# Second layer of a two-layer trunk: the order of the head pairs' rope transposes and of their attention, and TensorE's order by hand for all pairs

## The chip, the cores and the metric

The kernel runs on one core of a Trainium2 chip. The metric is the device time of one execution in microseconds (us). Three runs of the kernel before gave 768.90 to 769.38 us, median 769.24.

The engines have short names in the trace: PE is TensorE (matmuls and transposes), DVE is VectorE, ACT is ScalarE, POOL is GpSimd, SP issues DMAs.

## The reference

The program computes two layers of a sequence model on 512 tokens of width 1024. The first is a recurrent (mLSTM) layer with a memory cross-attention; the change does not touch it. The second is multi-head latent attention with 8 heads, again with a memory cross-attention. What matters here, of its core:

```python
kv = (rmsnorm(c_kv, kv_lat_norm) @ w_kv_b).reshape(bsz, s, B_HEADS, QK_NOPE + V_HEAD)   # 128 + 128
k = concat([k_nope, broadcast(k_pe)]); k = rmsnorm(k, k_gain)
k = concat([k[..., :QK_NOPE], rope(k[..., QK_NOPE:], positions)])
q = (rmsnorm(q_lat, q_lat_g) @ w_q_up).reshape(bsz, s, B_HEADS, QK_HEAD)                 # 128 + 64
q = rmsnorm(q, q_gain); q = concat([q[..., :QK_NOPE], rope(q[..., QK_NOPE:], positions)])
attn = chunk_causal_attention(q, k_sh, v_sh)       # blocks of 128 queries, chunk mask of 64
y_b = attn * silu(z)                               # z: a part of h @ w_in
x + concat([y_b, y_mem]) @ w_out
```

So each head's q and k has a part of 128 channels without position and a part of 64 channels that is rotated (rope).

## The kernel before

Products in float32 precision are made of three matmuls: an operand is split into a high part (ACT casts it, L130 or L133) and a low part (DVE subtracts, L131 or L134), and `prod` (L149 to L163) sums high x high, low x high (L157) and high x low (L162) in PSUM. Weights come by DMA into a buffer `wr` and are split into `wh` and `wl`, two buffers each. PSUM has four banks `acc` for products, two `att` for attention, two `tp` for transposes.

The second layer's heads are worked off in four pairs p = 0 to 3. `b_pair(p)` has three parts, and each yields between its steps. `b_kv(p)`: four products (one per 128 tokens, 6 matmuls of 512 columns) give k and v of two heads; DVE copies k (L928), ACT copies v and sums squares, and GpSimd makes the norm's factor and `krs`, the rotated part of k times that factor (L938). `b_q(p)`: four products of 9 matmuls of 384 columns; DVE copies the plain part (L978), ACT the part to be rotated into `qrs` (L979), and GpSimd rotates it in four operations on all tokens at once (L872 to L875) and makes `rqp`, the norm's factor as a power (L183). `b_z(p, c)` twice: the gate z, 24 matmuls of 512 columns in two halves of 12, then a silu. Between the steps of z six calls of `b_T` transpose on PE what attention needs: k and q of head 0 and 1 (L952) and the rope part of both heads (`h = 2`, L957). Each call takes one `tp` bank, which ACT and DVE read out; for the rope part each half takes one ACT operation (L960) and one or two of DVE (L962, L963).

`b_attn(p)` has nine steps: six of scores with softmax, for two heads and the query blocks (0, 1), (2) and (3); two steps after its scores a unit's probabilities are transposed (L1018); after the third unit of a head 20 value matmuls (L1031) and the gate. `weave(main, side, plan)` runs one step of main, then as many of side as the plan says.

The order on the engines comes from two sources. A scheduler sets it for all engines, except that inside `manual_schedule(engines={PE})` PE takes its instructions in the order in which the program writes them. Before, pairs 0 and 1 and the attention of pair 0 are outside of this block; pairs 2 and 3, the attention of pairs 1 to 3 and the out projection are inside. The four banks and the tile buffers are handed out by the scheduler as they come free.

Of the kernel before, what the change touches and what calls it, by code (L numbers as in the profile page):

```python
# [22 lines left out]
EPS = 1e-6  # L23
# [25 lines left out]
def chain(*gens):  # L49
    for g in gens:  # L50
        yield from g


def drain(g):
    for _ in g:
        pass
# [3 lines left out]
def trunk(ctx: ExitStack, tc: tile.TileContext, pv_d, pos_d, x_d, mem_d, memT_d, wmem_d, wg_d, wa_d, woa_d,  # L60
# [119 lines left out]
    def rpow(out, ss, mul, add, n):  # L180
        t = tiny([P, n])
        G.tensor_scalar(t, ss, mul, add, op0=ALU.mult, op1=ALU.add)  # L182
        G.tensor_tensor(out=out, in0=t, in1=mhalf[:, :n], op=ALU.pow)  # L183
# [721 lines left out]
    def b_z(p, c):  # L905
        d = pairs.setdefault(p, {})
        if c == 0:
            d["z"] = st([P, 2, S], ("z4", "mv")[p % 2])
        sz = d["z"]
        w = load(wb_d[8 + 2 * p + c], KT, P)  # L910
        ps = acc()
        yield from proj_T(w, hT, ps)
        silu2(sz[:, c], ps)
        yield

    def b_kv(p):
        d = pairs.setdefault(p, {})
        kns = st([P, NT, 256], "s4", 2)
        krs = s2([P, NT, P])
        d["v"] = vt = st([P, NT, 256], ("gt", "mkT")[p % 2])  # L920
        d["ks"] = kns, krs
        w = load(wkvb_d[p], 2, 512)
        ss = tiny([P, NT, 2])
        r2 = tiny([P, NT, 2])
        for t in range(NT):
            ps = acc()
            prod([(ps, lat(ckT, k, t), sub(w, slice(None), k), True) for k in range(2)], True, True)
            V.tensor_copy(kns[:, t], ps[:, 0:256])  # L928
            A.activation(vt[:, t], ps[:, 256:512], AF.Copy)
            for h in range(2):  # L930
                sqsum(kns[:, t, h * P:(h + 1) * P], ss[:, t, h:h + 1])
            if t < 3:
                yield
        V.tensor_tensor(out=ss, in0=ss, in1=sspe.unsqueeze(2).broadcast_to([P, NT, 2]), op=ALU.add)
        rpow(r2.rearrange("p a b -> p (a b)"), ss.rearrange("p a b -> p (a b)"), 1.0 / 192, EPS, 8)
        k4 = kns.rearrange("p t (h c) -> p t h c", h=2)
        V.tensor_tensor(out=k4, in0=k4, in1=r2.unsqueeze(3).broadcast_to([P, NT, 2, P]), op=ALU.mult)
        G.tensor_tensor(out=krs.rearrange("p t (h c) -> p t h c", h=2),  # L938
                        in0=kb.unsqueeze(2).broadcast_to([P, NT, 2, 64]),
                        in1=r2.unsqueeze(3).broadcast_to([P, NT, 2, 64]), op=ALU.mult)  # L940
        yield

    def b_T(p, name, h):

# [21 lines left out]
    def b_q(p):  # L966
# [6 lines left out]
        ssq = tiny([P, NT, 2])  # L973
        for t in range(NT):
# [7 lines left out]
            if t < 3:  # L982
                yield
        q4 = qrs.rearrange("p t (h c) -> p t h c", h=2)
        rope(q4, q4, 0, st([P, NT, 2, 64], "qt"),
             lambda i, a, b: tabs[:, i, :, a:b].unsqueeze(2).broadcast_to([P, NT, 2, b - a]))
        yield
        rpow(rqp.rearrange("p a b -> p (a b)"), ssq.rearrange("p a b -> p (a b)"), 1.0, 192 * EPS, 8)

    def b_attn(p):  # L990
        kn, qn, kh, qr, vt, sz, rqp = (pairs[p][n] for n in ("kn", "qn", "kr", "qr", "v", "z", "rq"))
# [53 lines left out]
            yield  # L1045

    def b_pair(p):
        yield from b_kv(p)
        yield from b_q(p)
        todo = [(n, h) for h in range(3) for n in "kq"]  # L1050
        for _ in chain(b_z(p, 0), b_z(p, 1)):
            yield
            b_T(p, *todo.pop(0))

    drain(b_pair(0))
    weave(b_pair(1), b_attn(0), (0,) * 5)
    x1b = []

    def residual():
# [6 lines left out]
        A.dma_start(out_d[t * P:(t + 1) * P, half * 512:(half + 1) * 512], o)  # L1066

    with tc.manual_schedule(engines={mybir.EngineType.PE}):
        weave(chain(*(b_pair(p) for p in range(2, 4)), residual(), out_proj(wob_d, yT, b_done)),
              chain(*(b_attn(p) for p in range(1, 4))), ((0,) * 5 + (1,) * 9) * 2)  # L1070


_OUTS = [((1, S, D), 'float32')]
# [101 lines left out]
```

## Time and profile before

| | |
|---|---|
| median of three runs | 769.24 us |
| the profiled execution | 769.35 us |
| its span, first to last instruction | 767.6 us |
| PE busy | 755.0 us, 98% |
| DVE, ACT, POOL busy | 63%, 53%, 14% |
| granted TensorE clock, mean | 1.0 |

The trace gives for every instruction its start and its duration. Matmuls overlap in the pipeline and their ends are modelled, so the time that one takes is read from start to start; a row of the timeline merges neighbours of one kind, with their count. An idle time in brackets is the time for which the engine stood before the row, and what released it.

The head pairs begin at about 538 us; the out projection begins at 685 us and ends the kernel.

### The profile page before, as it was taken

The numbers are of one execution on the slowest core, as the hardware profiler recorded it, in microseconds if no ns is written. First come the engines' busy times: TensorE is split into PE (matmuls) and PEld (weight loads), VectorE is DVE, ScalarE is ACT, GpSimd is POOL, SyncE is SP. The second block draws the span as 40 slices with busy tenths as digits, with TensorE's granted clock in tenths as the row PEclk, the third lists the DMA queues.
The fourth block names the chain that finished last, engine by engine and source line by source line (L and its number), as shares of the span: only waits on it lengthen the run. The fifth ranks groups of instructions, "written<-read, shape, count | busy, mean of one in ns | idle before, by whom it ended". The sixth has DMA issues, their size and how long they took to land.

```text
span 767.6 us, 10826 instructions
## 1 busy us (share of the span) xinstructions
PE 755.0 (98%) x3948; PEld 647.8 (84%) x3948; DVE 484.1 (63%) x945; ACT 409.4 (53%) x958; POOL 106.8 (14%) x159
## 2 busy tenths in 40 slices
PE   8999998999999999999999999999999999999998
PEld 6798887888888888888888887899888888888886
DVE  5743599547868836766434664566758697776422
ACT  6964557345446435536333658457856666644220
POOL 0131010010110101001001131020334230500000
PEclk9999999999999999999999999999999999999999
DMA  9523120322132222224443532121221111511241
GB/s 323 207 84 109 56 84 29 109 83 90 63 99 80 83 89 104 71 94 154 154 160 137 174 129 73 53 83 59 83 87 59 56 50 40 190 56 56 66 155 55
DMA packets 25909, 76.39 MB, mean 100 GB/s; under 512 B 3072, under 2 KB 3968, under 8 KB 25856
## 3 DMA queue, kind: packets, MB, share of 16 engines
q1 hardware_dynamic: 24144, 73.44, 28.4%
q10 hardware_dynamic: 1584, 2.25, 0.8%
q8 instruction: 31, 0.51, 0.3%
q14 instruction: 22, 0.18, 0.1%
q0 software_dynamic: 128, 0.01, 0.0%
HBM read 71.49 MB, written 4.19 MB: 99 GB/s over the span
## 4 chain that ended last, share of the span: by engine, by line
PE 85%; DVE 8%; ACT 3%; issue 1%; DMA 1%; POOL 0%; SPq 0%; ACTq 0%; DVEq 0%
PE acc L157 47%; PE acc L162 23%; PE att L157 3%; PE att L1031 2%; PE att L162 2%; DMA yTh<-in_wmem_dram 1%; DVE wl L131 1%; PE tp L1018 1%; DVE tiny L328 1%; ACT junk L187 1%; DVE kl L629 1%; ACT s L338 1%; PE tp L952 1%; PE att L715 1%; PE att L716 1%
## 5 line engine op out<-in xcount | busy, mean ns | idle before, releaser
L131 DVE TENSOR_TENSOR wl<-wr,wh 128x1024 fp32r<-128x1024 f32 (+5 forms) x117 | 136.2, 1165 | 152.9 <-ACT wh L130 126.7
L130 ACT ACTIVATE wh<-wr 128x1024 fp32r<-128x1024 f32 (+5 forms) x117 | 117.5, 1008 | 134.1 <-PE acc L157 123.8
L157 PE MATMUL acc<-wh,hTl 128*128 128x512 f32 (+3 forms) x320 | 113.3, 365 | 0.0
L157 PE MATMUL acc<-wh,hTh 128*128 128x512 f32 (+3 forms) x320 | 112.4, 367 | 0.3 <-ACT hTh L133 0.3
L157 PE MATMUL acc<-hTh,wh 128*128 128x512 f32 x256 | 101.8, 398 | 0.0
L157 PE MATMUL acc<-hTl,wh 128*128 128x512 f32 x256 | 100.3, 392 | 0.0
L157 PE MATMUL acc<-wh,yTh 128*128 128x512 f32 (+1 forms) x224 | 84.7, 382 | 0.0
L157 PE MATMUL acc<-wh,yTl 128*128 128x512 f32 (+1 forms) x224 | 84.5, 379 | 0.0
L162 PE MATMUL acc<-wl,hTh 128*128 128x512 f32 (+3 forms) x320 | 82.0, 364 | 0.0
L162 PE MATMUL acc<-hTh,wl 128*128 128x512 f32 x256 | 69.8, 392 | 0.0
L157 PEld LDWEIGHTS acc<-wh,hTh 128*128 128x128 f32 x320 | 59.1, 188 | 9.4 <-ACT hTh L133 0.6
L157 PEld LDWEIGHTS acc<-wh,hTl 128*128 128x128 f32 x320 | 59.6, 188 | 8.7 <-DVE hTl L134 0.2
L162 PEld LDWEIGHTS acc<-wl,hTh 128*128 128x128 f32 x320 | 56.5, 188 | 8.6
L162 PE MATMUL acc<-wl,yTh 128*128 128x512 f32 (+1 forms) x224 | 60.1, 378 | 0.0
L162 PEld LDWEIGHTS acc<-hTh,wl 128*128 128x128 f32 x256 | 47.6, 188 | 9.9 <-DVE wl L131 0.2
L157 PEld LDWEIGHTS acc<-hTh,wh 128*128 128x128 f32 x256 | 48.1, 188 | 9.1
L157 PEld LDWEIGHTS acc<-hTl,wh 128*128 128x128 f32 x256 | 48.2, 188 | 9.1
L157 PEld LDWEIGHTS acc<-wh,yTh 128*128 128x128 f32 x224 | 42.1, 188 | 7.2
L157 PEld LDWEIGHTS acc<-wh,yTl 128*128 128x128 f32 x224 | 42.1, 188 | 7.1
L162 PEld LDWEIGHTS acc<-wl,yTh 128*128 128x128 f32 x224 | 41.2, 188 | 7.4
L182 POOL TENSOR_SCALAR tiny<-tiny 128x8 f32<-128x8 f32 (+3 forms) x21 | 5.5, 262 | 245.1 <-ACT junk L187 68.2
L157 PE MATMUL acc<-wh,u 128*128 128x384 f32 (+1 forms) x160 | 37.8, 362 | 0.8 <-ACT u L133 0.7
(285 smaller groups left out, 1387.0 us busy)
## 6 DMA issues: line engine op xcount, KB each, us to landing
wr<-in_wa_dram SPq DMA_DIRECT2D x46, 512.0 KB, 3.2
wr<-in_wb_dram SPq DMA_DIRECT2D x16, 512.0 KB, 3.5
wr<-in_woa_dram SPq DMA_DIRECT2D x12, 512.0 KB, 3.2
wr<-in_wob_dram SPq DMA_DIRECT2D x12, 512.0 KB, 3.2
wr<-in_wmem_dram SPq DMA_DIRECT2D x8, 512.0 KB, 3.4
yTh<-in_wmem_dram SPq DMA_DIRECT2D x5, 512.0 KB, 7.3
yTl<-in_x_dram SPq DMA_DIRECT2D x4, 512.0 KB, 9.1
u<-in_x_dram SPq DMA_DIRECT2D x4, 512.0 KB, 6.2
```

The lines of the kernel that those rows point to most:

```text
L130: A.activation(hi, src, AF.Copy)
L131: V.tensor_tensor(out=lo, in0=src, in1=hi.bitcast(F32), op=ALU.subtract)
L157: PE.matmul(ps, x if lhs else w_[0], w_[0] if lhs else x, start=start and id(ps) not in seen, stop=False)
L162: PE.matmul(ps, a_[0] if lhs else w_[1], w_[1] if lhs else a_[0], start=False, stop=stop and left[id(ps)] == 0)
L187: A.activation(j[:, :src.shape[-1]], src, AF.Square, scale=scale, accum_out=accum)
L328: V.tensor_reduce(mx[:, j:j + 1], ps, axis=AX.X, op=ALU.max)
L338: A.activation(out[j], ps, AF.Exp, bias=nb[:, j:j + 1], scale=rq[:, j:j + 1], accum_out=sm[:, j:j + 1])
L629: V.scalar_tensor_tensor(out=u[:, d:], in0=raw[:, :S - d], scalar=col("cw", (3 - d) * 16 + j), in1=u[:, d:], op0=ALU.mult, op1=ALU.add)
L715: PE.matmul(ps[:, :258], low(c, i), v[0][:, c], start=False, stop=False)
L716: PE.matmul(ps[:, :256], ph[:, blk(c, i)], v[1][:, c], start=False, stop=c == i)
L952: PE.transpose(tp[:, t * P:(t + 1) * P], main[:, t, h * P:(h + 1) * P], ident)
L1031: PE.matmul(ps[:, i * P:(i + 1) * P], vt[:, c, h * P:(h + 1) * P], pTs[h][:, o:o + P], start=c == 0, stop=c == i)
```

## The change

The diff has four parts. In `b_kv` the `yield` moves ahead of the norm's two products, so that these belong to the step after; in `b_q` the power for `rqp` moves from behind the last yield to ahead of it. `b_pair` writes its steps as a plan: in pair 0 the four key/value steps, three z steps with the transposes of k, the four q steps, three z steps with the transposes of q; in pairs 1 to 3 key/value, q, and then six z steps with k and q in turn. In all of them the rope part (`h = 2`) is now transposed first. All pairs are inside the manual block, and the attention of a pair is woven into the next pair from its first step.

```diff
@@ b_kv
         V.tensor_tensor(out=ss, in0=ss, in1=sspe.unsqueeze(2).broadcast_to([P, NT, 2]), op=ALU.add)
         rpow(r2.rearrange("p a b -> p (a b)"), ss.rearrange("p a b -> p (a b)"), 1.0 / 192, EPS, 8)
+        yield
         k4 = kns.rearrange("p t (h c) -> p t h c", h=2)
...
-        yield
@@ b_q
+        rpow(rqp.rearrange("p a b -> p (a b)"), ssq.rearrange("p a b -> p (a b)"), 1.0, 192 * EPS, 8)
         yield
-        rpow(rqp.rearrange("p a b -> p (a b)"), ssq.rearrange("p a b -> p (a b)"), 1.0, 192 * EPS, 8)
@@ b_pair
-        yield from b_kv(p)
-        yield from b_q(p)
-        todo = [(n, h) for h in range(3) for n in "kq"]
-        for _ in chain(b_z(p, 0), b_z(p, 1)):
+
+        kv, q, z = b_kv(p), b_q(p), chain(b_z(p, 0), b_z(p, 1))
+        kT, qT = [("k", h) for h in (2, 0, 1)], [("q", h) for h in (2, 0, 1)]
+        if p == 0:
+            plan = [(kv, None)] * 4 + [(z, t) for t in kT] + [(q, None)] * 4 + [(z, t) for t in qT]
+        else:
+            plan = [(kv, None)] * 4 + [(q, None)] * 4 + [(z, t) for two in zip(kT, qT) for t in two]
+        for g, t in plan:
+            next(g, None)
+            if g is not kv:
+                drain(kv)
             yield
-            b_T(p, *todo.pop(0))
-
-    drain(b_pair(0))
-    weave(b_pair(1), b_attn(0), (0,) * 5)
+            if t:
+                b_T(p, *t)
+
     x1b = []
@@ the manual block
-        weave(chain(*(b_pair(p) for p in range(2, 4)), residual(), out_proj(wob_d, yT, b_done)),
-              chain(*(b_attn(p) for p in range(1, 4))), ((0,) * 5 + (1,) * 9) * 2)
+        drain(b_pair(0))
+        weave(chain(*(b_pair(p) for p in range(1, 4)), residual(), out_proj(wob_d, yT, b_done)),
+              chain(*(b_attn(p) for p in range(4))), (1, 1, 1, 1, 1, 0, 1, 0, 1, 0, 1, 0, 1, 0) * 3)
```

The three places at which PE's list moves most. First pair 0, the transposes of q's rope part (`tp_5423` from `s_930` before, `tp_5394` from `s_942` now). Before, they stand behind the key/value products of pair 1 and its first scores:

```order
L157 MATMUL acc_5483<-wh_5438,u_878_5059 128x512
L162 MATMUL acc_5483<-wl_5439,u_877_5058 128x512 x2
L157 MATMUL att_5628<-qk_5331,qk_5351 128x512
L162 MATMUL att_5628<-qk_5331,qk_5351 128x512
L957 MATMUL tp_5423<-ident,s_930_5236 128x128 x4
L157 MATMUL acc_5518<-wh_5505,u_895_5129 128x384
```

Now they stand behind the last q product (`acc_5351`) and the first half of a z product (`acc_5381`), whose eight first matmuls alternate as its first two do:

```order
L162 MATMUL acc_5351<-wl_5291,u_895_5129 128x384 x2
L162 MATMUL acc_5351<-wl_5297,u_896_5130 128x384
L157 MATMUL acc_5381<-hTh_3866,wh_5377 128x512
L157 MATMUL acc_5381<-hTl_3867,wh_5377 128x512
...
L162 MATMUL acc_5381<-hTh_3866,wl_5378 128x512 x4
L957 MATMUL tp_5394<-ident,s_942_5301 128x128 x4
L157 MATMUL acc_5381<-hTh_3866,wh_5377 128x512
```

Everything that lay between q's last product and these transposes, but for one half of z, now comes later.

Second, the end of a z step, here in the last pair before (`tp_6763` is attention's, `tp_6769` and `tp_6799` the rope parts of k and q, `att_6784` the values):

```order
L162 MATMUL acc_6725<-hTh_3866,wl_6722 128x512 x4
L1018 MATMUL tp_6763<-ident,s_1276_6685 128x128 x4
L957 MATMUL tp_6769<-ident,s_1190_6352 128x128 x4
L1031 MATMUL att_6784<-e_6690,gt_5895 128x128 x10
L957 MATMUL tp_6799<-ident,s_1218_6434 128x128 x4
L157 MATMUL acc_6817<-wh_6823,yTh_3868 128x512
```

And now the same pair (`tp_6709` is q's rope part, `tp_6722` attention's, `tp_6728` and `tp_6755` the first head's k and q):

```order
L162 MATMUL acc_6667<-hTh_3866,wl_6664 128x512 x4
L957 MATMUL tp_6709<-ident,s_1241_6525 128x128 x4
L1018 MATMUL tp_6722<-ident,s_1261_6610 128x128 x4
L952 MATMUL tp_6728<-ident,s_1189_6351 128x128 x4
L157 MATMUL acc_6742<-hTh_3866,wh_6738 128x512
```

Three groups of transposes follow on each other where there were two and a block of values.

Third, the start of pair 0: the latents' transposes (L864, three tiles) and what follows them. Before, q products (`acc_5238` and its neighbours) lie between the second and the third tile:

```order
L864 MATMUL tp_5139<-ident,s_888_5108 128x128
L157 MATMUL acc_5238<-wh_5225,u_895_5129 128x384
L157 MATMUL acc_5254<-wh_5225,u_895_5129 128x384
L157 MATMUL acc_5270<-wh_5225,u_895_5129 128x384
L157 MATMUL acc_5286<-wh_5225,u_895_5129 128x384
L864 MATMUL tp_5146<-ident,s_885_5105 128x128
```

Now the three tiles and k's rope part (`tp_5244`) follow on each other, behind the first half of z:

```order
L864 MATMUL tp_5139<-ident,s_888_5108 128x128
L864 MATMUL tp_5146<-ident,s_885_5105 128x128
L864 MATMUL tp_5146<-ident,s_886_5106 128x128
L864 MATMUL tp_5146<-ident,s_887_5107 128x128
L864 MATMUL tp_5146<-ident,s_888_5108 128x128
L957 MATMUL tp_5244<-ident,s_902_5156 128x128 x4
L157 MATMUL acc_5229<-hTh_3866,wh_5225 128x512
```

The q products of the pair have moved behind all of k's transposes.

## Rows read from the trace of the kernel before

**Rows 1.** The page's first part: engine, busy us, share of the span, instructions.

```profile
PE 755.0 (98%) x3948; PEld 647.8 (84%) x3948; DVE 484.1 (63%) x945; ACT 409.4 (53%) x958; POOL 106.8 (14%) x159
```

**Rows 2.** Windows, one stretch: length, busy PE, PEld, DVE, ACT, POOL; clock; DMA share, GB/s.

```profile
543.00:700.00 157.00, 154.87 (x894) 135.88 (x894) 119.49 (x264) 97.17 (x285) 42.23 (x36) 1.00 0.24 76
```

**Rows 3.** Timeline, PE, pair 0: start, us, line, operation, out<-in, shapes, count, [idle before].

```profile
543.50 1.09 PE L864 MATMUL tp<-ident,s 128*128 128x128 f32 x8
545.31 0.97 PE L157 MATMUL acc<-wh,u 128*128 128x384 f32 x4 [0.73 <-ACT u L133]
...
551.63 0.68 PE L162 MATMUL acc<-wl,u 128*128 128x384 f32 x3
...
571.91 0.60 PE L957 MATMUL tp<-ident,s 128*128 128x128 f32 x4
```

**Rows 4.** Timeline, GpSimd, pair 0; the last row is of pair 1.

```profile
549.12 2.08 POOL L938 TENSOR_TENSOR s<-m,tiny 128x512 f32<-128x512 f32 x1
554.50 1.03 POOL L872 TENSOR_TENSOR qt<-s,tabs 128x256 f32<-128x256 f32 x1 [3.29 <-ACT s L979]
555.48 0.74 POOL L873 TENSOR_TENSOR qt<-s,tabs 128x256 f32<-128x256 f32 x1
...
559.44 1.76 POOL L875 TENSOR_TENSOR s<-s,qt 128x512 f32<-128x512 f32 x1
...
589.21 1.28 POOL L875 TENSOR_TENSOR s<-s,qt 128x512 f32<-128x512 f32 x1
```

**Rows 5.** Timeline, PE: the first matmul of a z half, and what follows the half.

```profile
635.68 0.48 PE L157 MATMUL acc<-hTh,wh 128*128 128x512 f32 x1
...
638.52 0.49 PE L1018 MATMUL tp<-ident,s 128*128 128x128 f32 x3
```

**Rows 6.** Timeline, PE: the last three q matmuls of pairs 2 and 3.

```profile
618.82 0.68 PE L162 MATMUL acc<-wl,u 128*128 128x384 f32 x3
...
659.12 0.68 PE L162 MATMUL acc<-wl,u 128*128 128x384 f32 x3
```

**Rows 7.** Timeline, GpSimd, the rope of pairs 2 and 3.

```profile
622.95 0.73 POOL L872 TENSOR_TENSOR qt<-s,tabs 128x256 f32<-128x256 f32 x1 [8.96 <-ACT s L979]
...
627.21 1.39 POOL L875 TENSOR_TENSOR s<-s,qt 128x512 f32<-128x512 f32 x1
...
663.57 1.79 POOL L873 TENSOR_TENSOR qt<-s,tabs 128x256 f32<-128x256 f32 x1
...
668.68 1.32 POOL L875 TENSOR_TENSOR s<-s,qt 128x512 f32<-128x512 f32 x1
```

**Rows 8.** Timeline, ScalarE: a latent's split, two weight casts, the rope part's read-out.

```profile
545.43 0.69 ACT L133 ACTIVATE u<-tp,pv 128x512 fp32r<-128x512 f32 x1
...
620.05 2.01 ACT L130 ACTIVATE wh<-wr 128x1024 fp32r<-128x1024 f32 x2
...
685.43 1.21 ACT L960 ACTIVATE v<-tp 64x512 fp32r<-64x512 f32 x2 [2.33 <-DVE kl L963]
```

**Rows 9.** Timeline, VectorE: splits of latents, weights, and the rope part's read-out.

```profile
545.29 1.60 DVE L134 SCALAR_TENSOR_TENSOR u<-tp,pv,u 128x512 fp32r<-128x512 f32 x2 [0.40 <-ACT u L133]
...
558.82 1.23 DVE L131 TENSOR_TENSOR wl<-wr,wh 128x1024 fp32r<-128x1024 f32 x1 [3.24 <-ACT wh L130]
...
663.55 1.22 DVE L131 TENSOR_TENSOR wl<-wr,wh 128x1024 fp32r<-128x1024 f32 x1
...
682.95 0.68 DVE L1024 COPY e<-tp 128x512 f32<-128x512 f32 x1
...
687.22 0.68 DVE L963 TENSOR_TENSOR v<-tp,v 64x512 fp32r<-64x512 f32 x1
```

**Rows 10.** Timeline of PE at the program's start and end, and the last window.

```profile
1.81 4.34 PE L121 MATMUL tp<-ident 128*128 128x128 f32 x20 [1.81 <-POOL ident masks.py:199]
...
763.30 0.61 PE L162 MATMUL acc<-wl,yTh 128*128 128x512 f32 x2
...
767.00:767.60 0.60, 0.00 (x0) 0.00 (x0) 0.00 (x0) 0.00 (x0) 0.00 (x0) 0.50 0.00 0
```

## Prediction

> **What bounds the kernel now.** I read the page first: PE is busy for 98% of the span, the other engines for 14 to 63% [rows 1]. So the time is PE's work plus the stretches in which PE waits, and a change of order that leaves PE's work alone moves only the second. Next I took the stretch that the change touches, from the first key/value product of pair 0 (543 us) to the out projection (700 us): PE is busy for 154.87 of 157.00 us [rows 2]. At most 2.1 us of idle time can be won there; a little more hides in matmuls that start late inside a busy stretch. The largest single wait is 0.73 us, on the query latents' split before the first q products [rows 3]. The question is therefore not what the change removes but what it makes PE wait for, since PE takes its list strictly as written.
>
> **What moves, and what it waits for.** The matmuls, their shapes and the other engines' instructions stay the same in number; the lists of PE differ, and with them the places at which a late operand is felt. I walked PE's new list and asked at each transposition whether its operand and its PSUM tile are there. Four places fail.
>
> *Rope part of q, pair 0.* In the list before, PE reaches these transposes at 571.91 us, some 20 us after the last q product of the pair, 551.63 + 0.68 = 552.31 [rows 3]. The operand is made by ScalarE's copy (L979) and then four GpSimd operations with the `rqp` power in between; the last of them ends at 559.44 + 1.76 = 561.20, 8.9 us after that product [rows 4]. In the new list one half of a z product lies between: 12 matmuls, 638.52 - 635.68 = 2.84 us with 0.09 of the transposes ahead of it, so 2.75 [rows 5]. PE stands for 8.9 - 2.75 = 6.15 us, whether at the head of the half (its weights wait for the last q product) or behind it. The same chain measured from the last q product, 619.50 and 659.80 [rows 6], took 9.1 and 10.2 us in pairs 2 and 3 [rows 7]. Bounds: L872 and L875 took 1.03 and 1.76 us in pair 0 and 0.73 and 1.28 at their shortest [rows 4, 7], so 8.1 us is the least, and 10.2 the most: 5.35 to 7.45. The new list of GpSimd keeps the power between the rope's operations, so the earlier line in the program does not shorten the rope.
>
> *Rope part of q, pairs 1 to 3.* Here two halves of a z product (5.5 us), one group of three transposes and the four of k's rope part lie between; at the full clock a transpose takes 0.109 us, half of 4.34 / 20 [rows 10], so the seven take 0.76 and the whole 6.25 us. For the chain I take ScalarE's new list: the two weight casts for z start when the fourth of the last nine q matmuls has passed, some 0.8 us before the end, and between them and L979 stands the cast of one gated output. In pair 2 it was 2.9 us from the start of these casts, 620.05, to the first rope operation, 622.95 [rows 7, 8], with a softmax operation in that place; GpSimd then took 6.7 us in pair 0, from 554.50 to 561.20 [rows 4]. That is 2.9 - 0.8 + 6.7 = 8.8 us; pair 2 had 9.1, and I take 8.95. PE waits 2.7 us each, 8.1 us in all. Bounds 8.0 (8.8 less the same 0.8) and 10.2 us: 1.75 to 3.95 each.
>
> GpSimd's rope operation L873 took 0.74 us in pair 0, where VectorE was idle from 555.58 to 558.82, and 1.79 in pair 3, where VectorE's two-input subtraction began 0.02 us earlier [rows 4, 7, 9]. The Trainium skill, in SBUF — State Buffer, section Who interferes with whom, says that a VectorE instruction with two SBUF inputs and a GpSimd instruction that reads SBUF lock each other out of a shared port. The trace agrees with that here. By this rule a waiting PE soon leaves VectorE idle and the rope runs at its shortest; the chain would be 8.1 and 8.0 us, and the sum 0.8 + 3 x 0.95 = 3.7 us lower.
>
> *Third tile behind the q rope, pairs 1 to 3.* Behind the rope transposes stand two more groups (attention's four and k's first head) and there are two `tp` banks. The list before has the 20 value matmuls between such groups. The third group must wait until a bank is read out. For the rope's bank: ScalarE 0.6 us for the first half (two took 1.21 [rows 8]), VectorE 0.68, the copy of the attention tile that stands between 0.68, and 0.68 again for the second half [rows 9], 2.7 us with the gaps, less the 0.44 of the four transposes: 2.3 us. If the attention tile's bank comes free first: 1.6. I take 2.0 each, 6.0 in all; bounds 4.8 and 6.9.
>
> *Start of pair 0.* Half a z product moves ahead of the latents' transposes, but the q products that lay among those move behind them. The first eight transposes take both banks; the third tile waits for one ScalarE operation of 0.69 and one VectorE operation of 0.8 [rows 8, 9], 1.5 us. Then PE transposes k's rope part, whose product on GpSimd ended at 549.12 + 2.08 = 551.20 before [rows 4]; with the two latent splits gone from ScalarE's list ahead of it and a larger weight cast added, I put it at 550.4. PE comes there at 543.5 + 2.75 + 0.9 + 1.5 + 0.45 = 549.1 and waits 1.2 us. The second head of k waits 0.4 us for the bank of the rope part. Together 3.1 us, against the 0.73 us wait and some 0.2 us around it that go [rows 3]: +2.2. Bounds: with k's rope part there by 549.1 and no wait for the bank +0.6, at most +3.2.
>
> *The clock.* The granted clock was full in the whole stretch [rows 2]. At the end of the program it is at half (1.2 GHz of 2.4) from 767.0 us on, 3.1 us after the last matmul had ended (763.30 + 0.61) [rows 10]; at the start, after 1.81 us without a matmul, the 20 warm-up transposes took 4.34 us, where eight later ones took 1.09 [rows 3, 10]. The standstill in pair 0 is about 5 us long without a matmul in it. I expect the clock to be at half when PE resumes, and 4 us of work at half rate to lose 2.0 us; bounds 0 and 2.0. The other standstills are 1.2 to 2.7 us, shorter than the 3.1, and get nothing.
>
> *The rest.* The softmax waits of before, 2.13 - 0.73 = 1.4 us visible, may go, since attention now starts with the key/value steps. But there VectorE gets per step a copy, a softmax and the weights' low parts, about as much time as PE needs, so I let the same 1.4 us come back; bounds -2.1 and +4. Loads keep their order but for one z weight of pair 0 ahead of the q weights, and their buffers are free well before: 0.
>
> **The sum**, against the profiled execution's 769.35 us (0.1 us above the median of the runs shown): 6.15 + 8.1 + 6.0 + 2.2 + 2.0 + 0 = 24.45, so 793.8 us. All low bounds together give 5.35 + 5.25 + 4.8 + 0.6 + 0 - 2.1 = +13.9, all high ones 7.45 + 11.85 + 6.9 + 3.2 + 2.0 + 4 = +35.4.
>
> **Rivals.**
> 1. *Only pair 0 pays.* In pairs 1 to 3 ScalarE gets to L979 early, GpSimd is quick while PE stands, and the bank is free. For it: GpSimd's operations vary by a factor of two. Against it: the chain was never under 8.9 us in the rows, and PE has 6.25. Time: 769.35 + 6.15 + 2.2 + 2.0 = 779.7.
> 2. *The clock falls in the later pairs too.* Each has two standstills close together, 2.7 and 2.0 us with 0.9 us of transposes between. If these count as one, three more losses of 2.0 us come: 799.8. Against it: the only fall that the trace shows came after 3.1 us without any matmul.
> 3. *Not slower.* The operands of each transposition come in time, and the waits of before go: 769.35 - 2.1 = 767.2. This decides itself at one place: the q rope of pair 0 would have to be done within 2.75 us of the last q product. The four GpSimd operations alone took 6.7 us there [rows 4]. It could hold only if the new order of PE were not kept.
> 4. *VectorE falls behind in the key/value steps* and the softmax transposes wait, +4 us on top: 797.8.
>
> **How the numbers follow.** The forecast with its own bounds 0.57, rival 1 0.20, rival 2 0.11, rival 4 0.08, rival 3 0.03, and 0.01 for an end within 0.2%, about what a measurement of this kernel can tell from no change. A range from 780 to 801 leaves out half of rival 1, rival 3 and the tail above: under 0.2. Slower 0.95, same 0.02, faster 0.03.
>
> **What would show it.** Right: PE's longest wait is on the transposes of L957, released by GpSimd's L875, 5 to 7 us once and 2 to 3 us three times; the transposes of L952 behind them wait some 2 us for VectorE; PE's busy share falls to about 95%; the granted clock dips once near 570 us. Wrong: no wait of PE over 1 us at L957, or the rope's end less than 8 us behind the last q product. If waits of L1018 on VectorE lead the list, rival 4 was the larger part.

## The result and the profile after

The changed kernel took 803.88 us (median of four runs, 801.63 to 804.81) against 769.31 us (four runs, 768.90 to 769.45) of the kernel before on the same chip: ratio 1.044, 95% interval 1.0425 to 1.0455. The prediction was 793.8 us with a range of 780 to 801: slower, as forecast, but by 34.6 us where 24.5 were summed. The profiled execution took 804.81 us, its span is 803.0.

The page's first part answers to [rows 1], the row below it is the clock that PE was granted, in tenths, over 40 slices of the span:

```profile
PE 769.9 (96%) x3948; PEld 658.4 (82%) x3948; DVE 485.6 (60%) x945; ACT 410.3 (51%) x958; POOL 106.6 (13%) x159
PEclk9999999999999999999999999999898999979999
```

These two lines already split the loss. PE has as many instructions as before (3948), yet its busy time rose from 755.0 to 769.9: 14.9 us in which the same work ran more slowly. Its idle time rose from 767.6 - 755.0 = 12.6 to 803.0 - 769.9 = 33.1: 20.5 us of waits. Together they are the 35.4 us by which the span grew.

The waits, from the view that sums them for PE (line, what it waited for, us in total, times, longest):

```profile
PE tp L957 <- POOL s L875: 14.3, 4, 5.1
PE tp L952 <- DVE e L1024: 3.5, 3, 1.4
...
PE tp L952 <- DVE kl L963: 1.5, 1, 1.5
```

The first is q's rope part, once per pair; the second the third group of transposes in pairs 1 to 3; the last belongs to the start of pair 0. On the timeline of PE (start, us, row, [idle before]) pair 0 and pair 1 look like this:

```profile
548.46 0.66 PE L864 MATMUL tp<-ident,s 128*128 128x128 f32 x4 [1.46 <-DVE u L134]
549.50 0.65 PE L957 MATMUL tp<-ident,s 128*128 128x128 f32 x4 [0.38 <-POOL s L939]
...
556.45 0.63 PE L952 MATMUL tp<-ident,s 128*128 128x128 f32 x4 [1.52 <-DVE kl L963]
...
562.67 0.69 PE L162 MATMUL acc<-wl,u 128*128 128x384 f32 x3
563.88 0.50 PE L157 MATMUL acc<-hTh,wh 128*128 128x512 f32 x1 [0.52 <-ACT wh L130]
...
572.00 1.12 PE L957 MATMUL tp<-ident,s 128*128 128x128 f32 x4 [5.10 <-POOL s L875]
...
600.48 0.70 PE L162 MATMUL acc<-wl,u 128*128 128x384 f32 x3
...
611.35 0.69 PE L957 MATMUL tp<-ident,s 128*128 128x128 f32 x4 [3.33 <-POOL s L875]
612.43 1.08 PE L1018 MATMUL tp<-ident,s 128*128 128x128 f32 x4 [0.40 <-DVE kl L963]
614.50 1.11 PE L952 MATMUL tp<-ident,s 128*128 128x128 f32 x4 [0.98 <-DVE e L1024]
```

The same place in pairs 2 and 3 has 2.61 and 3.24 us at L957, and behind it 0.43 and 1.44 us in pair 2 and 1.07 in pair 3. Before, these transposes were reached without such a wait [rows 3]. GpSimd's rope of pair 1, which answers to [rows 4, 7], ends 10.1 us behind the last q product (600.48 + 0.70 to 609.05 + 2.24):

```profile
603.08 1.42 POOL L872 TENSOR_TENSOR qt<-s,tabs 128x256 f32<-128x256 f32 x1 [9.59 <-ACT s L979]
...
609.05 2.24 POOL L875 TENSOR_TENSOR s<-s,qt 128x512 f32<-128x512 f32 x1
```

The slower work is the clock's. The view of windows (length, busy PE, PEld, DVE, ACT, POOL; clock; DMA share, GB/s) shows the head pairs as a whole, against [rows 2], and then the five stretches at half clock:

```profile
543.00:735.00 192.00, 168.69 (x889) 145.02 (x888) 120.62 (x264) 97.26 (x286) 41.29 (x36) 0.91 0.19 62
550.40:553.81 3.41, 3.41 (x9) 2.66 (x9) 1.89 (x4) 0.90 (x2) 0.00 (x0) 0.50 0.01 2
570.88:577.71 6.83, 5.71 (x16) 4.66 (x17) 1.38 (x2) 2.02 (x3) 1.06 (x1) 0.50 0.00 0
611.84:618.67 6.83, 5.45 (x18) 4.21 (x17) 3.95 (x6) 1.87 (x3) 0.00 (x0) 0.50 0.02 9
659.63:666.46 6.83, 5.76 (x16) 4.70 (x17) 2.42 (x4) 1.28 (x2) 0.00 (x0) 0.50 0.00 0
704.00:714.24 10.24, 8.14 (x24) 6.22 (x25) 5.46 (x7) 1.87 (x3) 0.97 (x1) 0.50 0.15 53
```

PE was busy for 3.41 + 5.71 + 5.45 + 5.76 + 8.14 = 28.5 us at 1.2 GHz. If that work takes half as long at 2.4 GHz, 14.2 us were lost; by the starts of neighbouring 512-column matmuls, which lie 0.42 us apart at 617.5 and 0.23 us at 620.4, it is nearer 13. Either estimate explains nearly all of the 14.9 us. Each stretch begins within a series of the standstills shown or named above, or up to 0.9 us behind one.

```profile
617.12 0.63 PE L157 MATMUL acc<-hTh,wh 128*128 128x512 f32 x1
617.54 0.63 PE L157 MATMUL acc<-hTl,wh 128*128 128x512 f32 x1
...
620.36 0.39 PE L157 MATMUL acc<-hTl,wh 128*128 128x512 f32 x1
620.59 0.39 PE L157 MATMUL acc<-hTh,wh 128*128 128x512 f32 x1
```

### The profile page after: what moved, and what is told of

The parts are those of the page before. It is cut to its first block, busy times and chain, and to the rows that moved or that the text cites. A ratio compares the mean times of both kernels' runs of the same rounds, so it can differ in the third digit from the quotient of the medians.

```text
span 803.0 us, 10832 instructions
## 1 busy us (share of the span) xinstructions
PE 769.9 (96%) x3948; PEld 658.4 (82%) x3948; DVE 485.6 (60%) x945; ACT 410.3 (51%) x958; POOL 106.6 (13%) x159
## 4 chain that ended last, share of the span: by engine, by line
PE 84%; DVE 7%; ACT 3%; POOL 2%; DMA 2%; issue 1%; POOLq 0%; DVEq 0%; ACTq 0%
PE acc L157 46%; PE acc L162 23%; PE att L157 4%; PE att L1031 2%; PE att L162 2%; DVE wl L131 1%; ACT wh L130 1%; PE tp L952 1%; PE tp L1018 1%; DVE kl L629 1%; DMA wr<-in_wkvb_dram 1%; DVE tiny L328 1%; PE att L715 1%; PE att L716 1%; DMA yTh<-in_wmem_dram 1%
## 5 line engine op out<-in xcount | busy, mean ns | idle before, releaser
L157 PE MATMUL acc<-hTh,wh 128*128 128x512 f32 x256 | 106.8, 417 | 1.3 <-ACT wh L130 1.3
L157 PE MATMUL acc<-hTl,wh 128*128 128x512 f32 x256 | 104.7, 409 | 0.0
L162 PE MATMUL acc<-hTh,wl 128*128 128x512 f32 x256 | 71.7, 401 | 0.0
L157 PEld LDWEIGHTS acc<-hTh,wh 128*128 128x128 f32 x256 | 50.7, 198 | 12.3 <-ACT wh L130 2.6
L162 PEld LDWEIGHTS acc<-hTh,wl 128*128 128x128 f32 x256 | 50.1, 197 | 10.8
L157 PEld LDWEIGHTS acc<-hTl,wh 128*128 128x128 f32 x256 | 50.9, 199 | 9.8
```

The lines of the kernel that those rows point to most:

```text
L157: PE.matmul(ps, x if lhs else w_[0], w_[0] if lhs else x, start=start and id(ps) not in seen, stop=False)
L162: PE.matmul(ps, a_[0] if lhs else w_[1], w_[1] if lhs else a_[0], start=False, stop=stop and left[id(ps)] == 0)
```

## The experiments

Theory 1: PE, held to its written order, stands at q's rope part, at the third tile and at the start of pair 0, and these standstills also bring the clock down in every pair. Theory 2: the loss is in the waits, or in early attention, and the clock is beside the point. All ratios are to runs of the kernel before on the same chip. The expectations count the standstills at q's rope part somewhat longer than the rows above: 5.9 us in pair 0 and 10.9 in pairs 1 to 3, against 5.10 and 9.2.

| Run | median us | ratio (95%) | expected us |
|---|---|---|---|
| q's rope wait filled | 792.85 | 1.030 (1.028, 1.032) | 792 |
| all waits filled | 798.37 | 1.038 (1.036, 1.040) | 790 |
| half of it filled, pairs 1 to 3 | 804.75 | 1.046 (1.044, 1.047) | 794, or 800 to 804 |
| q's rope part last | 796.48 | 1.036 (1.034, 1.038) | 777 |
| early attention alone | 782.54 | 1.017 (1.016, 1.019) | 768 to 773 |
| no q rope | 792.11 | 1.029 (1.028, 1.031) | 776 |
| tile read out in one go | 790.11 | 1.028 (1.026, 1.030) | 780 |
| key/value weights elsewhere | 800.22 | 1.039 (1.036, 1.041) | 778 |
| attention one step later | 799.04 | 1.038 (1.036, 1.040) | 798 |
| pair 0 by the scheduler | 796.71 | 1.035 (1.033, 1.036) | 792.7 |
| middle order | 773.14 | 1.004 (1.003, 1.005) | 770.5 |
| before with one plan line | 769.75 | 1.0004 (0.9995, 1.0013) | 767.5 |
| the same, pair 2 later (two runs) | 772.08; 770.75 | 1.0025 (1.0015, 1.0036); 1.0006 (0.9997, 1.0015) | 767.8; 768.2 |
| the same, eight attention steps a pair | 776.35 | 1.0079 (1.0066, 1.0093) | 768 |

**What the clock costs.** The wait at q's rope part is filled with work:

```diff
@@ b_T
         tp = tps()
+        if (name, h) == ("q", 2):
+            for _ in range(46 if p == 0 else 28):
+                PE.transpose(tp[:, 0:P], ident, ident)
```

> The changed kernel with dummy 128x128 transposes of the identity matrix put directly ahead of q's rope transposes: 46 in pair 0 and 28 in each later pair, written into the same PSUM tile that the real ones then overwrite. They need nothing but a free tile, so TensorE works where it stood; the results are the same. By 0.109 us each they fill 5.0 of the 5.9 us standstill of pair 0 and 3.05 of the 3.2 to 3.9 us of the others. Theory 1 (the standstills on q's rope part also bring the clock down, and the half clock afterwards costs more than they do): the stretches of half clock that follow these four places go (6.83, 6.83, 6.83 and 10.24 us; about 3 us lost in each), only the short one near 550 us stays; 804 - 12 = 792 us, range 789 to 796. Theory 2 (the loss is in the waits, the clock is beside the point or follows the third tile's wait): the fillers replace idle time and the time stays at 803 to 806.

792.85 us, 11.0 less than the changed kernel, although the fillers only take the place of idle time. The clock stayed full in all four places (here pair 1, the window 605 to 620), and of the head pairs' stretches only the one at the start of pair 0 was left, 551.35 to 554.76.

```profile
605.00:620.00 15.00, 14.00 (x92) 12.16 (x91) 9.15 (x11) 6.17 (x9) 4.25 (x3) 1.00 0.09 31
```

So theory 1 holds for the clock, and the four later stretches are worth 11 us. In one of the four executions the mean granted clock was 1.000; it took 790.07 us. With the other waits filled as well:

```diff
@@ b_T
+        n = {("q", 2): 28, ("k", 0): 14}.get((name, h), 0) if p else {("q", 2): 46, ("k", 2): 4, ("k", 1): 12}.get((name, h), 0)
+        for _ in range(n):
+            PE.transpose(tp[:, 0:P], ident, ident)
@@ Latent.trans, third tile: 15 of the same
```

> As the run that fills q's rope waits, and dummy transposes as well in the waits for the third tile in pairs 1 to 3 (14 each) and at the start of pair 0 (15 in the latents' third tile, 4 ahead of k's rope part, 12 ahead of k's second head). Theory 1: the clock is full to the end; all standstills filled and no half clock gives 804 - 14 = 790 us, what is left over before (20 us) being the waits themselves. If the third tile's wait, and not q's rope part, were what brings the clock down, this run is well below the other (by 8 us or more); by theory 1 the two differ by 1 to 3 us. Theory 2: 803 to 806.

798.37 us: the clock was full in all the head pairs, but the time rose. The flaw was mine: a filler that writes into the tile must itself wait for the tile. At the third tile PE stood 0.78 us and then spent 1.5 us on the fillers on top (L952 is the fillers' line here):

```profile
613.62 1.75 PE L952 MATMUL tp<-ident 128*128 128x128 f32 x14 [0.78 <-DVE e L1029]
```

The 73 fillers at such places are 8.0 us at 0.109; without them the run would be at 790.4. Last, half of the filling, and none in pair 0 (lines stand 3 lower than in the change):

```diff
+            for _ in range(0 if p == 0 else 14):
```

> The changed kernel with 14 dummy transposes (1.5 us) ahead of q's rope transposes in pairs 1 to 3 alone: the standstills there fall from 2.8 to 3.5 us to some 1.3 to 2.0, those on the third tile behind them (1.3 to 1.6 us) and pair 0 stay as they are. If the first standstill by itself brought the clock down, a shorter one leaves it full in pairs 1 to 3: 804 - 10 = 794 us, range 791 to 796. If the two standstills count together (some 3.3 us without products instead of 5), the clock still falls there: 800 to 804 us.

804.75 us, not faster at all, and the clock fell in all four pairs (6.83 us in pair 0; 3.41, 6.83 and 6.83 in pairs 1 to 3). In pair 1:

```profile
608.56 0.66 PE L960 MATMUL tp<-ident,s 128*128 128x128 f32 x4 [0.82 <-POOL s L875]
610.89 0.63 PE L1021 MATMUL tp<-ident,s 128*128 128x128 f32 x4 [1.68 <-DVE kl L966]
612.96 1.11 PE L955 MATMUL tp<-ident,s 128*128 128x128 f32 x4 [1.44 <-DVE e L1027]
```

Two things follow. Standstills of 0.8 to 1.7 us with only transposes between them can be enough for a fall. In pair 1 it came at 612.53, within the third; in pairs 2 and 3 it came within the second, or at its end (656.90 and 704.69; the second standstills, 1.68 and 1.69 us, end at 657.48 and 704.65). Single standstills of 1.82 to 2.18 us in pairs 1 to 3 of the run with early attention alone, and of 2.30 us in pair 3 of the run with the tile read out in one go, left the clock full. That speaks for their counting together, which was the prediction's rival 2, though a series of short standstills does not always end in a fall (see the last section). And the 1.68 us at L1021 were 0.40 in the changed kernel: the first wait had covered most of the second.

**What stands behind the wait on q's rope.** First q's rope part is put last:

```diff
-        kT, qT = [("k", h) for h in (2, 0, 1)], [("q", h) for h in (2, 0, 1)]
+        kT, qT = [("k", h) for h in (2, 0, 1)], [("q", h) for h in (0, 1, 2)]
```

> The changed kernel with one edit: of q's three groups of transposes the rope part comes last instead of first (k's rope part still comes first). Theory 1: two more halves of z products (5.5 us) and two groups of transposes then cover the chain of ScalarE and GpSimd behind the last q product. Pair 0 keeps under 1 us of its 5.9 us, pairs 1 to 3 none of their 10.9, and the half clock behind them goes (about 12): 804 - 5.3 - 10.9 - 11 = 777 us, range 773 to 783. Rival (the early weave of attention, with its three groups of transposes on two tiles and VectorE's work per step, is what costs): the waits only move to the next group, 792 us or more.

796.48 us, the rival's case: the wait on GpSimd is down to 1.8 us in all, but attention's transposes, the third group behind k's rope part and first head, now wait for the bank of k's rope part, 10.8 us in pairs 1 to 3, with half clock around it (6.83, 6.83, 3.41 us). In pair 2:

```profile
653.20 1.09 PE L1018 MATMUL tp<-ident,s 128*128 128x128 f32 x4 [4.07 <-DVE kl L963]
```

The same with GpSimd's work left out (the query's rope part is not rotated):

```diff
@@ b_q
-        rope(q4, q4, 0, st([P, NT, 2, 64], "qt"),
-             lambda i, a, b: tabs[:, i, :, a:b].unsqueeze(2).broadcast_to([P, NT, 2, b - a]))
```

> The changed kernel without q's rotary product: the four GpSimd operations per pair between the last q product and q's rope transposes are left out (the query's rope part goes on unrotated), everything else stays. Theory 1 (these operations are what TensorE stands for): the waits on q's rope part, 5.9 us in pair 0 and 10.9 in pairs 1 to 3, go, and with them the half clock behind them (about 12). What is late next is the bank of k's rope part, which in the run with q's rope last took 6.6 us from transposes to release; with GpSimd out of VectorE's way I put the wait for it at 1.5 to 2.5 us in pairs 1 to 3 each, against the 1.8 of the third tile there now. 804 - 5.9 - 10.9 - 12 + 1 = 776 us, range 773 to 783. Rival (ScalarE's copy and its queue are what is late, GpSimd comes on top only): waits of 2 us and more stay at q's rope part, 787 us or more.

792.11 us. No wait on q's rope part is left: without the four GpSimd operations the operand is there in time. But the waits behind it grew from 1.4 to 4.4 us (pair 1), and the clock fell again in pairs 1 to 3. The lines stand 2 higher here:

```profile
601.95 0.63 PE L1016 MATMUL tp<-ident,s 128*128 128x128 f32 x4 [2.92 <-DVE kl L963]
604.01 1.11 PE L952 MATMUL tp<-ident,s 128*128 128x128 f32 x4 [1.44 <-DVE e L1022]
```

Of the 28 us expected, 12 came. Why that bank is late is on ScalarE's timeline of the changed kernel: between the read-outs of the two halves of k's rope tile stands the cast of the next pair's key/value weights, and it waits for their load.

```profile
605.29 0.59 ACT L960 ACTIVATE v<-tp 64x512 fp32r<-64x512 f32 x1
607.86 1.06 ACT L130 ACTIVATE wh<-wr 128x1024 fp32r<-128x1024 f32 x1 [1.98 <-DMA wr<-in_wkvb_dram]
608.94 0.59 ACT L960 ACTIVATE v<-tp 64x512 fp32r<-64x512 f32 x1
```

So, on top of q's rope last, the tile is read out in one go:

```diff
@@ b_T (hv: the two halves)
...
+        for h, hs, other in hv:
+            A.activation(r[hs, h], tp[hs], AF.Copy)
+        for h, hs, other in hv:
+            V.tensor_tensor(out=(kl[hs, h] if name == "k" else r[other, h]), in0=tp[hs], in1=r[hs, h].bitcast(F32),
+                            op=ALU.subtract)
+        if name == "k":
+            for h, hs, other in hv:
+                V.tensor_copy(r[other, h], r[hs, h])
```

> The run with q's rope transposed last, and the rope tile read out in one go: ScalarE's two copies, then VectorE's two subtractions, and only then VectorE's two copies of k's high parts into the other half (they do not read the tile). Theory 1 now says that there TensorE waits for the bank of k's rope part, 10.8 us in pairs 1 to 3, since its release hangs on the second half, behind a weight cast that itself waits for TensorE. Read out in one go the bank is free some 2.5 to 3 us earlier: 796.5 - 3 x 2.7 - 8 (the half clock of 6.83, 6.83 and 3.41 us behind these waits) = 780 us, range 776 to 787. Rival (VectorE is simply behind by then, or the wait moves on to the next group): 792 us or more.

790.11 us. The wait for k's rope bank is gone, and the next group took it over: 10.0 us in pairs 1 to 3 on VectorE's L1026 (line 1024 of the change), since the same cast now stands ahead of the following read-outs. In pair 1:

```profile
604.36 1.11 PE L952 MATMUL tp<-ident,s 128*128 128x128 f32 x4 [3.87 <-DVE e L1026]
```

Then the load is taken out of that place, on top of the run just shown (pair 0 keeps its `load`; `hi` and `lo` are two new tiles):

```diff
@@ b_kv, p > 0
-        w = load(wkvb_d[p], 2, 512)
...
+            for k in range(2):
+                raw, c_ = s2(), slice(k * 512, (k + 1) * 512)
+                nc.sync.dma_start(raw, wkvb_d[p][:, c_])
+                split(hi[:, c_], lo[:, c_], raw)
...
```

> The run with the rope tile read out in one go, and the key/value weights of pairs 1 to 3 loaded into two 2 KB buffers of the pool of small tiles instead of the pair of weight buffers. In the changed kernel and in that run ScalarE's cast of these weights stands ahead of the read-outs of the next tiles, and at 607.86 and 599.86 us it waits 2.0 and 1.8 us for their load, which could start only when VectorE had read the first z weight; VectorE's part then stands behind the cast, and the read-outs behind both. Theory 1: with the load early the cast does not hold the read-outs up; the 10.0 us wait for the third group falls to 3 us or less, and the half clock (6.83 and 3.41 us) goes: 790 - 7 - 5 = 778 us, range 775 to 784. Rival (the two engines are behind by their own work, whatever the load does): 787 us or more.

800.22 us: the sum was wrong, the mechanism right for pairs 1 and 2, where the third group's wait fell from 3.87 to 1.1 us. In pair 3 the next weights are the out projection's, which are still loaded the old way, and there the wait is 3.88 us. But PE now waited for the key/value weights themselves, 1.94 us ahead of pair 1 and 2.59 ahead of pairs 2 and 3, and the clock fell behind that. Here L961 is L952 of the change, and L1035 is L1024:

```profile
605.51 0.66 PE L961 MATMUL tp<-ident,s 128*128 128x128 f32 x4 [1.13 <-DVE e L1035]
...
617.83 0.73 PE L157 MATMUL acc<-wh,u 128*128 128x512 f32 x2 [2.59 <-ACT wh L130]
...
703.83 0.66 PE L961 MATMUL tp<-ident,s 128*128 128x128 f32 x4 [3.88 <-DVE e L1035]
```

Ahead of pair 2 these weights' loads were issued between 600.80 and 604.73 us and took at most 3.6 us to land; their casts ran long after that, at 617.15 and 618.42, behind the read-out of q's rope part in ScalarE's order:

```profile
615.94 1.18 ACT L969 ACTIVATE v<-tp 64x512 fp32r<-64x512 f32 x2
617.15 0.63 ACT L130 ACTIVATE wh<-s 128x512 fp32r<-128x512 f32 x1
```

**The third tile, early attention, pair 0.** Attention's transposes moved by one step:

```diff
-              chain(*(b_attn(p) for p in range(4))), (1, 1, 1, 1, 1, 0, 1, 0, 1, 0, 1, 0, 1, 0) * 3)
+              chain(*(b_attn(p) for p in range(4))), (1, 1, 1, 1, 1, 0, 1, 0, 1, 0, 0, 1, 1, 0) * 3)
```

> The changed kernel with one edit: in each of pairs 1 to 3 attention's seventh-step transposes are taken one step later, behind half a z product, so that the q rope transposes are followed by one group instead of two. Theory 1: the third tile's wait (5.7 us in all) goes; the wait on q's rope part stays, and with it most of the half clock: 804 - 5.7 = 798 us, range 794 to 800. If the half clock came from the sequence of two standstills a few transposes apart, it goes too and the time is 788 us or less. Rival (the wait moves elsewhere): 802 us or more.

799.04 us, in the expected range, but by luck. The third tile's wait went, and a new one of 1.68 us came at the second group in pairs 1 and 3, so that PE's idle time fell only from 33.1 to 32.5 us; its busy time fell from 769.9 to 765.1, most of that by less half clock. In pairs 1 and 3 PE stood 2.35 and then 1.68 us, and the clock fell; in pair 2 it stood 2.61 and 0.43 us, and the clock stayed full:

```profile
611.28 0.66 PE L957 MATMUL tp<-ident,s 128*128 128x128 f32 x4 [2.35 <-POOL s L875]
613.61 0.66 PE L952 MATMUL tp<-ident,s 128*128 128x128 f32 x2 [1.68 <-DVE kl L963]
...
657.94 0.66 PE L957 MATMUL tp<-ident,s 128*128 128x128 f32 x4 [2.61 <-POOL s L875]
659.02 0.63 PE L952 MATMUL tp<-ident,s 128*128 128x128 f32 x4 [0.43 <-DVE kl L963]
```

```profile
612.81:619.64 6.83, 6.03 (x17) 4.81 (x18) 3.47 (x5) 1.28 (x2) 0.00 (x0) 0.50 0.10 29
653.00:667.00 14.00, 10.96 (x62) 8.95 (x61) 9.49 (x12) 6.36 (x10) 4.76 (x4) 1.00 0.13 44
```

Next, the kernel before with the weave and TensorE's order of the change, and its own order inside the pairs:

```diff
@@ before
-    drain(b_pair(0))
-    weave(b_pair(1), b_attn(0), (0,) * 5)
@@ the manual block: as in the change
```

> The kernel before with one part of the change: attention is woven in from the next pair's first step on and TensorE's order is written by hand for all four pairs, but each pair keeps its old order (rope parts transposed last, z products and transposes behind the q products, old places of the powers). Theory 1 (the rope parts' place is what costs): within 3 us of before, 768 to 773 us, with the third tile's waits of up to 2 us in pairs 1 to 3 in the upper end. Rival (the early weave or the hand order of pairs 0 and 1 costs): 780 us or more.

782.54 us, over the expected range, as the rival had it. So 13 us come with early attention and the order by hand alone, without any fall of the clock. The third of three groups of transposes in a row waits 1.8 to 2.2 us in each of pairs 1 to 3, and the first scores of each of pairs 0 to 2 wait 1.0 to 1.3 us for q's rope part, which comes last there; in pair 1:

```profile
601.75 0.66 PE L952 MATMUL tp<-ident,s 128*128 128x128 f32 x4 [1.82 <-DVE e L1024]
...
614.45 0.39 PE L1004 MATMUL att<-v,v 128*128 128x256 f32 x1 [1.26 <-DVE v L963]
```

The change, then, has its rope parts first so that early scores find them; what it pays there is the chain that makes them. Then the changed kernel with pair 0 given back to the scheduler:

```diff
+    drain(b_pair(0))
     with tc.manual_schedule(engines={mybir.EngineType.PE}):
-        drain(b_pair(0))
```

> The changed kernel with pair 0 left to the scheduler instead of TensorE's order by hand; pairs 1 to 3 stay as changed. Theory 1: the start of pair 0 costs what it did before (2.9 us less), its short fall of the clock goes (1.7) and the 5.9 us stand on q's rope part with its half clock (3.4) shrink, since other products go ahead of it; 1.5 to 3 us of it come back at the first scores, as in the run with the middle order (2.6 us): 804 - 2.9 - 1.7 - 5.9 - 3.4 + 2.6 = 792.7 us, range 789 to 797. Rival (the order by hand in pair 0 is not what costs there): 800 us or more.

796.71 us, 7.2 less. The start of pair 0 was free of waits, but the scheduler too reached q's rope part early (2.68 us), and a stretch of 3.41 us at half clock remained.

**Towards a faster version.** The middle order keeps the old order inside each pair, leaves pair 0 to the scheduler and has this plan from pair 1 on:

```diff
+              ... (0, 1, 1, 1, 1, 1, 1, 0, 1, 0, 0, 1, 0, 1) * 3)
```

> Meant to beat before: the old order inside each pair (rope parts last, z products behind the q products), pair 0 left to the scheduler as before, TensorE's order by hand from pair 1 on, attention started one step after the next pair's first step (so that the first scores come two key/value products behind q's rope transposes), its last transposes one step later and its last value products between the last two groups, so that never three groups of transposes stand in a row. Theory: the waits of the run with early attention alone go (third tile 2.0 us and first scores 1.4 us in each of pairs 1 to 3, 2 us at the start): 782.5 - 6 - 4 - 2 = 770.5 us, range 767 to 774; no fall of the clock. Rival (early attention overloads VectorE in the key/value steps whatever the order): 777 us or more.

773.14 us. Early attention as such need not cost: the two waits of the run with early attention alone were gone. What was left over is one wait of 2.61 us at the first scores of pair 0, on q's rope part, and 3.41 us of half clock behind it. The smallest edit, on the kernel before:

```diff
-              chain(*(b_attn(p) for p in range(1, 4))), ((0,) * 5 + (1,) * 9) * 2)
+              chain(*(b_attn(p) for p in range(1, 4))), (0, 1, 1, 1, 1, 0, 1, 1, 1, 0, 0, 1, 0, 1) * 2)
```

> Meant to beat before: the kernel before with one line changed, the weave plan of pairs 2 and 3. Attention starts after the pair's second key/value step instead of after its sixth step, pauses one step so that scores of the third step are through when their transposes come, takes its first value products ahead of the first z half, and never puts three groups of transposes in a row. Before lost 3.3 us to waits there. In the run with the middle order what was left in these pairs were 0.43 us twice a pair, which this plan covers: 769.5 - 2 = 767.5 us, range 766 to 770. Rival (VectorE falls behind in the key/value steps): 772 us or more.

769.75 us, the same as before. In pairs 2 and 3 nearly all waits went (PE is busy for 84.85 of 85.00 us from 615 us on, against 84.03 before), but 2.4 us came up at their entrance, again q's rope part of the pair ahead and the first scores:

```profile
615.00:700.00 85.00, 84.85 (x500) 75.63 (x499) 63.89 (x155) 50.91 (x149) 22.56 (x18) 1.00 0.26 88
```

Two more plans start attention later in pair 2, `(0, 0, 0, 1, 1, 1, 1, 1, 1, 0, 0, 1, 1, 1)` and `(0, 0, 1, 1, 1, 1, 1, 1, 1, 0, 0, 1, 0, 1)`:

> As the run with one plan line changed, but in pair 2 attention starts behind the fourth key/value step (pair 3 as in that run: behind the second). There the first scores of pair 2 waited 1.9 us for q's rope part of pair 1; here two more key/value products, 2.7 us, lie between. Theory: that wait goes and nothing takes its place: 769.7 - 1.9 = 767.8 us, range 766.5 to 769. Rival (the wait moves to the value products or to the transposes): 769.5 us or more.

> As the run before in this call, attention of pair 2 starting behind the third key/value step: one product, 1.4 us, covers most of the 1.9 us. Theory: 768.2 us, range 767 to 769.5.

772.08 and 770.75 us: missed. Pair 1's rope transposes are outside the block, and in all three of these traces the scheduler has put them shortly ahead of the first scores, so the wait moved along (3.0 and 1.8 us at L1004; behind the 3.0 us there are 3.41 us of half clock). A third plan, `(0, 0, 1, 1, 1, 1, 0, 1, 1, 0, 0, 1, 0, 1)` for both pairs, leaves out one of attention's nine steps per pair until too late and so does not compute the layer; its 776.35 us, where 768 were expected, say nothing about the order. No version beat the kernel before.

## Why the prediction missed its range

- *What bounds the kernel, and what the change does to it*: right. PE has the same instructions, and its written order makes it wait at the four kinds of places that were named.
- *Rope part of q, pair 0* (6.15 us): right. PE stood 5.10 us, and 0.52 more for the half's weights.
- *Rope part of q, pairs 1 to 3* (8.1 us): 3.33 + 2.61 + 3.24 = 9.2 us, inside the bounds. The chain took 9.4 to 10.1 us where 8.95 were taken. The Trainium skill's rule of the shared port (SBUF — State Buffer, section Who interferes with whom) would have made the sum lower, if a waiting PE leaves VectorE idle. It did not here: L872 took 1.42 us, while VectorE's two-input subtractions of weights and gated outputs filled 601.55 to 605.05. In pair 1, while PE stood (608.02 to 611.35), VectorE subtracted the next weights from 608.95 on, and L875, which began 0.10 us later, took 2.24 us, against 1.26 in pair 0:

```profile
601.55 2.35 DVE L131 TENSOR_TENSOR wl<-wr,wh 128x1024 fp32r<-128x1024 f32 x2
603.82 1.23 DVE L131 TENSOR_TENSOR yTl<-s,yTh 128x512 fp32r<-128x512 f32 x1
...
608.95 1.23 DVE L131 TENSOR_TENSOR wl<-wr,wh 128x1024 fp32r<-128x1024 f32 x1 [1.90 <-ACT wh L130]
```

- *Third tile* (6.0 us): 0.40 + 0.98, 0.43 + 1.44 and 1.07, 4.3 us, under the low bound of 4.8. PE's longer stand at q's rope covered part of it: with that stand cut to 0.82 us, the two waits behind it were 1.68 and 1.44 us in pair 1.
- *Start of pair 0* (2.2 us): 1.46 + 0.38 + 1.52 - 0.73 = 2.6 us. Right in size, but at k's second head rather than at k's rope part (whose forecast wait, 550.4 less 549.1, is 1.3 us and not 1.2, which changes nothing).
- *The rest* (0): the waits of before largely went and did not come back, 1.3 us to the good: the places above sum to 21.8 us, the idle time grew by 20.5. That VectorE would fall behind (rival 4) did not show.
- *The clock* (2.0 us, bounds 0 and 2.0): this is the step that failed. It cost 14.9 us. The fall forecast in pair 0 came, with 5.71 us of work at half rate where 4 were taken. The term put the start of pair 0 and pairs 1 to 3 at nothing, since it let a standstill count only by its own length, against the one example of 3.1 us at the program's end [rows 10]. There the runs showed 3.41, 5.45, 5.76 and 8.14 us of work at half rate. Two of the standstills in pairs 1 to 3 had become longer than that example, 3.33 and 3.24 us, but even so the comparison did not hold: in pair 3 the clock fell at 704.00, 2.2 us into this standstill:

```profile
705.02 1.12 PE L957 MATMUL tp<-ident,s 128*128 128x128 f32 x4 [3.24 <-POOL s L875]
```

And with half the filling it fell behind 0.82 and 1.68 us with transposes between. Rival 2 named that mechanism, but with a chance of 0.11 and 2.0 us each. Half of the 25.1 us of busy time in the four later stretches is 12.5 us, of which the run with q's rope wait filled gave 11.0 back.

With 14.9 in place of 2.0 the forecast's sum would be 806.7 us, 1.9 above the profiled execution; all waiting terms together, 22.45 us, were right to within 2. In part that is luck: the later pairs' rope waits were 1.1 us too low, the third tile's 1.7 too high. It is chance, too, that all high bounds together give the 35.4 us by which the span grew: they hold 4 us for the rest and 2.0 for the clock.

## What to carry to other kernels

A standstill of a bound engine is paid twice if its clock falls: count the standstills of a stretch together when only short work lies between them, take a fall there as likely rather than certain, and price each one by the length of half rate that other rows show, not by the wait. Waits nest: behind the first late operand stands the next one, which it had covered, so undoing one cause brings back less than it shows; walk the list on past the first wait, and into the in-order lists of the engines that release the next buffer. A fixed order helps only where each operand's chain is shorter than the work ahead of it: for a chain of 8.6 to 10.1 us, as here, that has to be counted in products.

## What was not expected of the hardware

Half clock came in stretches of 3.41, 6.83 or 10.24 us. One standstill of 2.61 us behind the last transposes of pair 0 was followed by a fall in the run with the middle order, and in the run with attention one step later a standstill of 2.61 us with 0.43 us behind it was not.

The same standstills need not have the same outcome. At the start of pair 0, 1.46 and 0.37 to 0.38 us stand in eight of the profiles: the clock fell in four (the changed kernel, q's rope wait filled, q's rope part last, attention one step later) and not in the other four. In the first layer, which no edit touches, standstills of 0.66 to 0.71, 0.40 to 0.42 and 0.83 to 0.84 us stand close together in all 17 profiles, with products between them; in four (q's rope wait filled, all waits filled, pair 0 by the scheduler, the second of the two later plans) 3.41 us of half clock follow, 128.09 to 131.51 in the first of these. The clock (the number behind the busy times) was at half there in that run, and full at the same place in the changed kernel:

```profile
128.09:131.50 3.41, 3.41 (x14) 2.92 (x13) 2.65 (x6) 1.15 (x3) 0.00 (x0) 0.50 0.00 0
```

```profile
128.00:131.40 3.40, 3.40 (x19) 2.91 (x20) 3.36 (x10) 2.61 (x6) 0.00 (x0) 1.00 0.00 0
```

So the lengths of the standstills alone do not decide it, and what does is not shown. Such a fall, some 1.7 us by half of 3.41, is also as large as what separates the last few plans from the kernel before. Nor was it settled by a run whether the load of the key/value weights alone, without a new wait, would free the third group in the changed kernel itself.
